# Sending the output stores of a batched matmul through the queue of its loads, and copying its sums out bank by bank

## The chip, the cores and the metric

One core of a Trainium2 chip. The metric is the device time of one execution in microseconds (us), as a median over runs. All runs compared here are fast: no execution was over 1.5% longer than the fastest of its kernel. One execution per run of each kernel was also profiled, and the traces are of those. The span of a profile is 1.8 us shorter than the time of its execution.

## The reference

```python
batch, m, k, n = 32, 512, 1024, 768
x      = randn(batch, m, k)   # float32
weight = randn(batch, k, n)   # float32
out    = np.matmul(x, weight) # float32
```

167.8 MB are read and 50.3 MB written, so there are 218.1 MB to move. Nothing is used twice.

## The kernel before

Loads go through GpSimd's (POOL) software queue, which casts float32 to bfloat16 on the way (a batch's 2048 KB of `x` land as 1024 KB, its 3072 KB of weights as 1536 KB). Stores go through SP's hardware queue, except those of the three batches before the last, which are held back behind all loads. The 128x128 blocks of `x` are transposed on PE.

```python
    CHUNKED = {B - 4: (4, 4), B - 3: (4, 4), B - 2: (4, 4), B - 1: (4, 2, 2)}
    HELD = {B - 4, B - 3, B - 2}
    # ... pools: w 5, x 5, xT 8, out 5 buffers; sums: 2 tiles of three PSUM banks ...

    def load_x(b):
        xs[b] = x_pool.tile([P, MT, K], BF16, name="x_sb")
        nc.gpsimd.dma_start(out=xs[b], in_=x_view[b])
    # ... load_w(b) the same, in the chunks of CHUNKED ...

    def evacuate(b, pair, pm):
        o = outs[b]
        nc.scalar.copy(o[:, pair * N2:pair * N2 + 1024], pm[:, 0:1024])
        nc.vector.tensor_copy(o[:, pair * N2 + 1024:(pair + 1) * N2], pm[:, 1024:N2])

        for b in range(B):              # loads of batches 0 to 3 were issued before
            if b + 4 < B:
                load_x(b + 4)
                load_w(b + 4)
            outs[b] = out_pool.tile([P, MT * N], F32, name="out_sb")
            if b not in CHUNKED:
                # ... transposes, matmuls, evacuate of two pairs of row tiles ...
                nc.sync.dma_start(out_view[b], outs[b])
                continue
            # ... last four batches: in the last chunk of batch b, the transposes
            #     of batch b + 1 stand between its matmuls ...
                        evacuate(b, pair, pms[pair])
                        if b not in HELD:       # the last batch: two half stores
                            cols = slice(pair * N2, (pair + 1) * N2)
                            nc.sync.dma_start(out_view[b, :, cols], outs[b][:, cols])
            if b in HELD:
                nc.gpsimd.dma_start(out=out_view[b], in_=outs[b])
```

## Time and profile before

| before | |
|---|---|
| time | 520.1 us, median of 3 (519.97 to 521.08) |
| span of the profile | 518.8 us |
| PE busy | 425.6 us (82%) |
| DMA work, 218.1 MB at the 428.2 GB/s of mid-span (428.9 with the instruction fetches) | 509.3 us |

The page's rows for the whole span: the busy tenths of the DMA engines in 40 slices, the two queues, and the transfers with their size and the median time from issue to landing.

```profile
DMA  8999999999999999999999999999999999999996
...
q0 software_dynamic: 10368, 88.61, 79.3%
q1 hardware_dynamic: 4320, 45.61, 21.2%
...
w_sb<-in_weight_dram POOLq DMA_DIRECT2D x28, 1536.0 KB, 63.1
out_dram<-out_sb SPq DMA_DIRECT2D x28, 1536.0 KB, 14.5
...
out_dram<-out_sb POOLq DMA_DIRECT2D x3, 1536.0 KB, 17.1
out_dram<-out_sb SPq DMA_DIRECT2D x2, 768.0 KB, 3.5
```

The DMA row is at its highest digit in all but the first and the last slice: this kernel is bound by the DMA engines. (The page's chain of work that ended last runs 80% through PE.) Queue 0 carries the loads (and the three held stores), queue 1 the other stores. A store that shares the engines with loads takes 14.5 us to land; a half store of the last batch, alone, takes 3.5.

The table of windows gives the same for stretches of time. The columns are the stretch, its length, busy time and instructions of PE, PEld, DVE, ACT and POOL, the clock granted to PE, the DMA share, and the GB/s written by the engines (a load counts with its bfloat16 bytes here).

```profile
core 0: us, PE busy (x) PEld busy (x) DVE busy (x) ACT busy (x) POOL busy (x), PEclk, DMA share, GB/s
260.00:300.00 40.00, 33.10 (x201) 21.93 (x203) 10.91 (x17) 6.08 (x6) 2.63 (x5) 0.96 1.02 261
500.00:505.00 5.00, 5.00 (x33) 3.09 (x32) 1.85 (x3) 1.01 (x1) 0.53 (x1) 1.00 0.99 412
505.00:510.00 5.00, 4.95 (x31) 3.04 (x31) 0.00 (x0) 0.00 (x0) 0.00 (x0) 1.00 0.87 369
510.00:515.00 5.00, 2.12 (x14) 1.08 (x12) 1.38 (x2) 2.02 (x2) 0.00 (x0) 1.00 0.41 168
515.00:518.80 3.80, 0.00 (x0) 0.00 (x0) 0.00 (x0) 0.00 (x0) 0.00 (x0) 0.61 0.58 238
```

In mid-span the share is 1.02, so there is no gap to fill. In the last 14 us it falls to 0.87, 0.41 and 0.58. The same stretch in finer slices (40 slices of 505 to 520 us, 0.375 us each):

```profile
DMA  9999898996563541200000698979999960000000
GB/s 393 393 459 459 360 459 360 492 459 295 229 262 164 229 197 66 98 0 0 0 0 0 262 426 360 492 311 475 393 426 426 360 262 0 0 0 0 0 0 0
```

The engines run out of held stores one after the other, all stand still for about 1.7 us, and then the last half stores run. By the packets of the trace, the last held store ends at 511.79 us on the slowest engine and the first half-store packet starts at 513.45: 1.66 us are lost even on the slowest engine.

The list of waits (engine, line, what it waited for: us in total, times, longest):

```profile
DVE out_sb L90 <- ACT out_sb L89: 157.7, 36, 8.4
...
PE pm L78 <- DMA w_sb<-in_weight_dram: 58.3, 21, 5.2
```

PE waits for weights because DMA bounds it. VectorE's long wait for ScalarE (one three-bank tile is copied out by both) is on an engine with time to spare (busy 124.2 of 518.8 us).

### The profile page before, as it was taken

Reading aid. Unit: us, or ns where it says so; the run is one execution under the profiler, and the core shown is the slowest. Engines: PE = TensorE matmul, PEld = TensorE weight load, DVE = VectorE, ACT = ScalarE, POOL = GpSimd, SP = SyncE. Lnnn points to the kernel's source line nnn. Section 1 sums busy time; section 2 is a strip of 40 time slices with the busy share of each in tenths; the row PEclk is TensorE's granted clock in tenths of the full one; section 3 lists DMA queues with packets and bytes.
Section 4 is the critical chain, followed back from the end, with each engine's and each line's share of the span. In section 5 each row is a group of like instructions: output and inputs, shape, how many; then the busy total and the mean of one; then the engine's idle time right before and its main releaser. Section 6 shows DMA issues by size and latency. Waiting matters only on the chain.

```text
span 518.8 us, 5796 instructions
## 1 busy us (share of the span) xinstructions
PE 425.6 (82%) x2512; PEld 278.3 (54%) x2560; DVE 124.2 (24%) x192; ACT 66.1 (13%) x65; POOL 38.9 (7%) x78
## 2 busy tenths in 40 slices
PE   1788789788888878897888978788887879878994
PEld 1455456455555545564555645466554555555662
DVE  1122222222221212212122122122221221223331
ACT  0011111011110101110011101011010110101111
POOL 4000000000000000000000000000000000001000
PEclk9999899798998979998899989799898997998998
DMA  8999999999999999999999999999999999999996
GB/s 159 216 231 268 269 265 277 275 239 272 254 275 278 253 270 241 275 279 273 253 250 262 275 279 247 268 250 275 277 252 273 242 273 278 265 266 229 215 329 250
DMA packets 14713, 134.59 MB, mean 259 GB/s; under 512 B 1632, under 2 KB 1632, under 8 KB 3040
## 3 DMA queue, kind: packets, MB, share of 16 engines
q0 software_dynamic: 10368, 88.61, 79.3%
q1 hardware_dynamic: 4320, 45.61, 21.2%
q8 instruction: 20, 0.33, 0.2%
q14 instruction: 5, 0.04, 0.0%
HBM read 167.77 MB, written 50.33 MB: 420 GB/s over the span
## 4 chain that ended last, share of the span: by engine, by line
PE 80%; another core or an unknown queue 10%; DMA 3%; issue 2%; ACT 2%; DVE 1%; POOL 0%; DVEq 0%; POOLq 0%
PE pm L78 70%; PE pt L64 11%; DMA w_sb<-in_weight_dram 3%; ACT out_sb L89 2%; DVE xT L66 1%; DVE out_sb L90 0%; POOL x_sb L50 0%; DVEq L66 0%; POOLq L152 0%
## 5 line engine op out<-in xcount | busy, mean ns | idle before, releaser
L78 PE MATMUL pm<-w_sb,xT 128*128 128x256 bf16 (+1 forms) x2000 | 372.4, 341 | 72.6 <-DMA w_sb<-in_weight_dram 58.3
L78 PEld LDWEIGHTS <-xT 128*128 128x128 bf16 x2048 | 207.6, 102 | 211.8 <-issue 56.5
L66 DVE COPY xT<-pt 128x1024 bf16<-128x1024 bf16 x128 | 85.2, 686 | 232.0 <-PE pt L64 232.0
L89 ACT COPY out_sb<-pm 128x1024 f32<-128x1024 f32 x64 | 64.8, 1013 | 446.3 <-PE pm L78 446.3
L64 PE MATMUL pt<-ident,x_sb 128*128 128x128 f32 x512 | 80.2, 291 | 13.9 <-DMA x_sb<-in_x_dram 12.5
L64 PEld LDWEIGHTS pt<-ident,x_sb 128*128 128x128 f32 x512 | 76.6, 207 | 21.6 <-issue 15.0
L90 DVE COPY out_sb<-pm 128x512 f32<-128x512 f32 x64 | 44.0, 687 | 157.7 <-ACT out_sb L89 157.7
L56 POOL DMA_DIRECT2D w_sb<-in_weight_dram x37 | 19.7, 531 | 239.2 <-DMA w_sb<-in_weight_dram 204.2
L50 POOL DMA_DIRECT2D x_sb<-in_x_dram x32 | 17.1, 536 | 196.8 <-PE pt L64 133.1
L137 POOL DMA_DIRECT2D out_dram<-out_sb x3 | 1.6, 533 | 29.2 <-DVE out_sb L90 29.2
L89 ACT ACT_TABLE_LOAD x1 | 1.3, 1283 | 0.7 <-PEq L152 0.7
masks.py:199 POOL TENSOR_SCALAR_AFFINE_SELECT ident<-ident 128x128 f32<-128x128 f32 x1 | 0.3, 287 | 0.1
masks.py:197 POOL MEMSET ident<- 128x128 f32 x1 | 0.2, 243 | 0.0
L152 POOL MEMSET const-float32-0.0<- 128x1 f32 x1 | 0.1, 99 | 0.2 <-issue 0.2
L152 POOL MEMSET const-bfloat16-1.0<- 128x1 bf16 x1 | 0.1, 102 | 0.0
L152 POOL MEMSET const-uint8-127<- 128x1 uint8 x1 | 0.1, 102 | 0.0
L152 POOL MEMSET const-float32-1.0<- 128x1 f32 x1 | 0.1, 99 | 0.0
## 6 DMA issues: line engine op xcount, KB each, us to landing
w_sb<-in_weight_dram POOLq DMA_DIRECT2D x28, 1536.0 KB, 63.1
out_dram<-out_sb SPq DMA_DIRECT2D x28, 1536.0 KB, 14.5
x_sb<-in_x_dram POOLq DMA_DIRECT2D x32, 1024.0 KB, 62.1
w_sb<-in_weight_dram POOLq DMA_DIRECT2D x7, 768.0 KB, 48.1
out_dram<-out_sb POOLq DMA_DIRECT2D x3, 1536.0 KB, 17.1
out_dram<-out_sb SPq DMA_DIRECT2D x2, 768.0 KB, 3.5
w_sb<-in_weight_dram POOLq DMA_DIRECT2D x2, 384.0 KB, 29.4
```

What stands on the lines that cost most here:

```text
L50: nc.gpsimd.dma_start(out=xs[b], in_=x_view[b])
L56: nc.gpsimd.dma_start(out=ws[b][:, at:at + n, :], in_=w_view[b, :, at:at + n, :])
L64: nc.tensor.transpose(pt[:, j, :], pairs[:, mt, j::JT], ident)
L66: nc.vector.tensor_copy(xT.rearrange("p j m r -> p (j m r)"), pt.bitcast(BF16).rearrange("p j m -> p (j m)"))
L78: nc.tensor.matmul(pm[:, half * N + off:half * N + off + size], xT[:, ko // 2, :, ko % 2], ws[b][:, ko, off:off + size], start=(ko == 0 an ...
L89: nc.scalar.copy(o[:, pair * N2:pair * N2 + 1024], pm[:, 0:1024])
L90: nc.vector.tensor_copy(o[:, pair * N2 + 1024:(pair + 1) * N2], pm[:, 1024:N2])
L137: nc.gpsimd.dma_start(out=out_view[b], in_=outs[b])
L152: nc = _bacc.Bacc("TRN2", target_bir_lowering=False, num_devices=1)
```

## The change

The intent is one queue that feeds the DMA engines in a fixed order: each store except the last batch's stands in the loads' queue, behind the load three batches ahead: the iteration of batch `b` issues the loads of `b + 3` and then the store of `b - 1`. For that, out buffers go from 5 to 7, load buffers from 5 to 4 and the look-ahead from four batches to three. The three-bank sum becomes three one-bank tiles, copied out by three copies.

```diff
-    HELD = {B - 4, B - 3, B - 2}
+    AHEAD = 3
-    ... w bufs=5, x bufs=5, out bufs=5
+    ... w bufs=4, x bufs=4, out bufs=7
+    def banks():
+        return [mpsum.tile([P, 512], F32, name=f"pm{i}") for i in range(3)]
 ... SPLITS and the matmuls' output name a bank and a column in it ...
     def evacuate(b, pair, pm):
-        o = outs[b]
-        nc.scalar.copy(o[:, pair * N2:pair * N2 + 1024], pm[:, 0:1024])
-        nc.vector.tensor_copy(o[:, pair * N2 + 1024:(pair + 1) * N2], pm[:, 1024:N2])
+        o = outs[b][:, pair * N2:(pair + 1) * N2]
+        nc.scalar.copy(o[:, 0:512], pm[0])
+        nc.vector.tensor_copy(o[:, 512:1024], pm[1])
+        nc.scalar.copy(o[:, 1024:N2], pm[2])
 ...
         for b in range(B):
-            if b + 4 < B:
-                load_x(b + 4)
-                load_w(b + 4)
+            if b + AHEAD < B:
+                load_x(b + AHEAD)
+                load_w(b + AHEAD)
+            if b > 0:
+                nc.gpsimd.dma_start(out=out_view[b - 1], in_=outs[b - 1])
 ...
-                nc.sync.dma_start(out_view[b], outs[b])
                 continue
 ...
-                        if b not in HELD:
+                        if b == B - 1:
 ...
-            if b in HELD:
-                nc.gpsimd.dma_start(out=out_view[b], in_=outs[b])
```

More of the change, by code (lines that the diff above doesn't have):

```diff
@@ L29 @@
     CHUNKED = {B - 4: (4, 4), B - 3: (4, 4), B - 2: (4, 4), B - 1: (4, 2, 2)}
-    HELD = {B - 4, B - 3, B - 2}
+    AHEAD = 3
     const = ctx.enter_context(tc.tile_pool(name="const", bufs=1))
-    w_pool = ctx.enter_context(tc.tile_pool(name="w", bufs=5))
-    x_pool = ctx.enter_context(tc.tile_pool(name="x", bufs=5))
+    w_pool = ctx.enter_context(tc.tile_pool(name="w", bufs=4))
+    x_pool = ctx.enter_context(tc.tile_pool(name="x", bufs=4))
     xT_pool = ctx.enter_context(tc.tile_pool(name="xT", bufs=8))
-    out_pool = ctx.enter_context(tc.tile_pool(name="out", bufs=5))
+    out_pool = ctx.enter_context(tc.tile_pool(name="out", bufs=7))
     tpsum = ctx.enter_context(tc.tile_pool(name="tpsum", bufs=2, space=bass.MemoryType.PSUM))
@@ L69, in transpose @@
         return xT
-    SPLITS = (((0, 512), (512, N - 512)), ((0, 1024 - N), (1024 - N, N2 - 1024)))
+    SPLITS = (
+        ((0, 0, 0, 512), (1, 0, 512, N - 512)),
+        ((1, N - 512, 0, 1024 - N), (2, 0, 1024 - N, N2 - 1024)),
+    )
     def matmuls(pm, half, xT, b, kos, together):
         for ko in kos:
-            for i, (off, size) in enumerate(SPLITS[half]):
+            for i, (bank, at, off, size) in enumerate(SPLITS[half]):
                 shares = half == 1 and i == 0
                 nc.tensor.matmul(
-                    pm[:, half * N + off:half * N + off + size],
+                    pm[bank][:, at:at + size],
                     xT[:, ko // 2, :, ko % 2],
@@ L96 @@
         make_identity(nc, ident)
-        for b in range(1, 4):
+        for b in range(1, AHEAD):
             load_x(b)
@@ L109 @@
                 for pair in range(2):
-                    pm = mpsum.tile([P, N2], F32, name="pm")
+                    pm = banks()
                     for half in range(2):
@@ L117 @@
                     evacuate(b, pair, pm)
-                nc.sync.dma_start(out_view[b], outs[b])
                 continue
             xT = ready.pop(b, None) or {mt: transpose(b, mt) for mt in range(MT)}
-            pms = [mpsum.tile([P, N2], F32, name="pm") for _ in range(2)]
+            pms = [banks() for _ in range(2)]
             at = 0
```

## The prediction

> **What bounds the kernel now.** The DMA engines, nearly everywhere. The page's DMA line reads 9 tenths in all slices but the first (8) and last (6); the table of windows gives a share of 1.02 to 1.03 in each 40 us stretch from 20 to 460 us. PE is busy 82% and waits 58.3 us for weights (list of waits). By packet sizes in the trace, counting a load by its float32 source bytes (twice what lands as bf16), the engines read about 428 GB/s wherever loads (first queue) and stores (second queue) mix. Loads alone reach 425 to 428 (4 to 30 us, 482 to 497 us); stores alone, held ones on the loads' queue, 405 to 420 (499 to 508 us), 0.46 us per 12 KB packet against 0.472 on the second queue. So mixing two queues costs nothing that separating could give back: 218.1 MB at 428 GB/s is 509.6 us of the 518.8 us span; the first packet starts at 2.6 us.
>
> **What lies outside that.** About 5 to 7 us, nearly all at the end. The held stores are done at 512.2 us, the last batch's half stores are issued at 512.6 and 513.9 us and land at 515.9 and 517.8 us: DMA share 0.87 (505 to 510), 0.41 (510 to 515), 0.58 after. But the engines are skewed: the 16 engines' landings of one late load spread over 3.5 to 6.4 us, and the slowest engine works until about 511.5 us. On it only 1.5 to 2 us is idle.
>
> **What the change does.**
> - Bytes, packets and matmuls are unchanged. 28 stores move from SP's queue to POOL's: 28 issues of 0.53 us on an engine 7% busy. [...] (a store beside loads lands after 14.5 us, though its bytes need 3.7 us alone).
> - The software queue has eight completion semaphores; weight loads are issued as the weights four batches back land. With three transfers per batch, eight in flight are 2.7 batches, about 42 us of DMA work: the queue should not run dry, although store b waits on POOL for batch b's evacuation.
> - Order: when the last weights land, 27 stores are done instead of 28, so they land about 3.7 us earlier, and four held stores (15 us) cover the last matmuls. The tail's idle time goes; the slowest engine gains its 1.5 to 2 us.
> - Evacuation by PSUM bank lets VectorE (0.69 us) go without waiting for ScalarE (1.01 us): up to 1 us before the last store, which now queues beside held stores anyway. The 157.7 us that VectorE waits for ScalarE are off the path.
> - Against: [...] POOL may be held by a wait.
>
> Net: minus 1 to 3 us for the tail, plus 0 to 3 for bubbles. I predict 518.3 us, 514.5 to 521.5; faster by over 2%: 0.02, within 2%: 0.94, slower: 0.04.
>
> **What would show it.** DMA share still 1.02 in mid-span; about 428 GB/s by source bytes; the last weights land near 497 us instead of 501; no 0.41 dip at the end; stores take 40 us or more to land; PE's wait for weights still about 58 us; VectorE's wait for ScalarE gone.
>
> **What would make it wrong.** The queue running dry because eight transfers or POOL's waits delay the next load; a mid-span rate below 420 GB/s because loads and stores no longer overlap in an engine; or above 432 because they no longer interfere; skew between engines growing or shrinking.

## The result, and the profile after

After: 517.88 us, median of 4 (517.62 to 518.26); before, on the same chip, 520.08 us. The ratio is 0.9954, 95% interval 0.9937 to 0.9971. (A ratio is the mean time of one kernel's fast runs over that of the other's of the same rounds, so it is not quite the ratio of the medians quoted.) Two later repetitions of after gave 517.70 (ratio 0.9938) and 518.00 us (0.9956). The predicted 518.3 us was near, and the class "within 2%" is right.

The page's rows for the whole span:

```profile
DMA  8999999999999999999999999999999999999996
...
q0 software_dynamic: 14400, 132.65, 99.9%
q1 hardware_dynamic: 288, 1.57, 0.7%
...
out_dram<-out_sb POOLq DMA_DIRECT2D x31, 1536.0 KB, 41.9
w_sb<-in_weight_dram POOLq DMA_DIRECT2D x28, 1536.0 KB, 43.2
...
out_dram<-out_sb SPq DMA_DIRECT2D x2, 768.0 KB, 7.0
```

Nearly everything is now on queue 0. A store takes 41.9 us from issue to landing, because it stands behind a load three batches ahead. The queue does not run dry: the DMA share is 1.02 to 1.03 in each 40 us stretch from 20 to 460 us. The trace bears out the prediction's eight: the landings of queue 0 are told on eight semaphores (99 to 106) and come in the order of issue, before and after, and counted at each issue there are never more than eight transfers in flight on it, the one issued included. In before there are eight at each issue from 5.6 to 479.2 us, and a weight load of mid-span is issued 0.53 us after the weights four batches back have landed; in after there are eight at each issue from 44.2 to 483.7 us. The last half stores take 7.0 us instead of 3.5: they are issued at 506.06 and 507.35 us, and held stores run beside them until 511.2 us.

The table of windows:

```profile
260.00:300.00 40.00, 34.52 (x212) 22.81 (x215) 9.89 (x15) 6.45 (x11) 4.25 (x8) 0.96 1.02 256
500.00:505.00 5.00, 4.95 (x32) 3.05 (x32) 0.00 (x0) 0.27 (x1) 0.00 (x0) 1.00 1.01 430
505.00:510.00 5.00, 1.70 (x11) 0.80 (x9) 1.38 (x2) 2.02 (x4) 0.00 (x0) 0.92 0.93 391
510.00:515.00 5.00, 0.00 (x0) 0.00 (x0) 0.00 (x0) 0.00 (x0) 0.00 (x0) 0.50 0.40 165
515.00:516.50 1.50, 0.00 (x0) 0.00 (x0) 0.00 (x0) 0.00 (x0) 0.00 (x0) 0.50 0.00 0
```

The finer slices of 505 to 520 us:

```profile
DMA  9996699989989795664232110000000000000000
GB/s 393 459 393 262 262 426 393 475 344 459 442 344 524 311 492 213 262 262 180 98 131 98 82 82 16 0 0 0 0 0 0 0 0 0 0 0 0 0 0 0
```

The gap is gone. The share of 510 to 515 us is still low (0.40, where the prediction expected no such dip), but it is no standstill. The long slope from 510 us on is the difference between the engines: the 16 landings of one late weight load are spread over 4.6 us here (3.8 us before), and the last digits belong to the slowest engines, which do not pause.

The waits:

```profile
DVE out_sb L97 <- PE pm L85: 116.2, 36, 8.5
...
PE pm L85 <- DMA w_sb<-in_weight_dram: 61.9, 23, 5.2
POOL w_sb L59 <- DMA out_dram<-out_sb: 56.5, 18, 3.2
```

VectorE no longer waits for ScalarE, and PE's wait for weights is about the same (61.9 against 58.3 us): this fits a copying out that is off the path, which e1 tests. GpSimd now waits 56.5 us for stores to land before it issues loads, and the DMA share does not fall for it (1.02 in 260 to 300 us, as before).

Two things in the trace were not in the prediction. First, counting a load by its source bytes (bfloat16 packets doubled, instruction fetches of 0.7 GB/s included), the engines move 430.3 GB/s between 60 and 450 us where they moved 428.9 before. Second, the program ends later after its last data packet: 2.24 us against 1.38. The end of the kernel, before and after, is a group of semaphore and drain instructions of one line; durations are min/median/max in ns, then the first and last start. Before:

```profile
L163 POOLq EVENT_SEMAPHORE  x4: 17/17/17, 518.1 to 518.7; - x4
L163 POOLq DRAIN  x3: 46/102/11436, 503.8 to 518.5; - x3
L163 SPq DRAIN  x3: 7/7/7, 518.0 to 518.3; - x3
```

After:

```profile
L170 POOLq EVENT_SEMAPHORE  x4: 17/17/17, 515.8 to 516.4; - x4
L170 POOLq DRAIN  x3: 46/95/18397, 497.3 to 516.2; - x3
L170 SPq DRAIN  x3: 7/7/7, 514.7 to 516.0; - x3
```

Before, SP has seen all stores land and drains at 518.0 us, and GpSimd follows at once (518.1): the last store ends the program. GpSimd's own long drain had ended at 503.77 + 11.44 = 515.2 us. After, SP is through at 514.7 us, but GpSimd's drain (from 497.34, 18.40 us long) ends only at 515.7, and the closing semaphores start at 515.8. The program's end has a new wait.

### The profile page after: what moved, and what is told of

Its sections match the earlier page's. It is cut to its first block, busy times and chain, and to the rows that moved or that the text cites. A ratio compares the mean times of both kernels' runs of the same rounds, so it can differ in the third digit from the quotient of the medians.

```text
span 516.5 us, 5888 instructions
## 1 busy us (share of the span) xinstructions
PE 424.2 (82%) x2512; PEld 277.7 (54%) x2560; DVE 127.0 (25%) x192; ACT 76.3 (15%) x129; POOL 53.9 (10%) x106
## 4 chain that ended last, share of the span: by engine, by line
DMA 74%; PE 21%; DVE 2%; issue 1%; ACT 0%; POOL 0%; POOLq 0%
DMA w_sb<-in_weight_dram 37%; DMA out_dram<-out_sb 24%; PE pm L85 19%; DMA x_sb<-in_x_dram 13%; PE pt L67 2%; DVE xT L69 1%; DVE out_sb L97 1%; ACT out_sb L98 0%; POOL x_sb L53 0%; POOLq L53 0%; POOLq L59 0%; POOLq L159 0%
## 5 line engine op out<-in xcount | busy, mean ns | idle before, releaser
L85 PE MATMUL pm<-w_sb,xT 128*128 128x256 bf16 (+1 forms) x2000 | 370.7, 340 | 66.6 <-DMA w_sb<-in_weight_dram 61.9
L96 ACT COPY out_sb<-pm 128x512 f32<-128x512 f32 x64 | 37.5, 586 | 287.9 <-PE pm L85 284.5
L98 ACT COPY out_sb<-pm 128x512 f32<-128x512 f32 x64 | 37.5, 586 | 142.4 <-PE pm L85 142.2
L53 POOL DMA_DIRECT2D x_sb<-in_x_dram x32 | 17.1, 536 | 192.6 <-DMA w_sb<-in_weight_dram 141.8
L59 POOL DMA_DIRECT2D w_sb<-in_weight_dram x37 | 19.7, 532 | 114.2 <-DMA out_dram<-out_sb 56.5
L115 POOL DMA_DIRECT2D out_dram<-out_sb x31 | 16.6, 536 | 136.8 <-DMA x_sb<-in_x_dram 64.7
## 6 DMA issues: line engine op xcount, KB each, us to landing
out_dram<-out_sb POOLq DMA_DIRECT2D x31, 1536.0 KB, 41.9
```

The costliest lines, as they stand in the source:

```text
L59: nc.gpsimd.dma_start(out=ws[b][:, at:at + n, :], in_=w_view[b, :, at:at + n, :])
L85: nc.tensor.matmul(pm[bank][:, at:at + size], xT[:, ko // 2, :, ko % 2], ws[b][:, ko, off:off + size], start=(ko == 0 and not (together an ...
L96: nc.scalar.copy(o[:, 0:512], pm[0])
L98: nc.scalar.copy(o[:, 1024:N2], pm[2])
L115: nc.gpsimd.dma_start(out=out_view[b - 1], in_=outs[b - 1])
```

## The experiments

The theory to test is that the gain is made of (a) the tail: stores deferred behind loads let PE finish earlier and cover its last work, worth the 1.66 us of idle time; and (b) a slightly higher rate in mid-span; while (c) the wait for GpSimd's drain takes part of it back. (c) was added after the runs e5 to e7. Rivals are the evacuation by bank, the buffers and look-ahead, and the tail alone.

All but the first of after were timed in 5 rounds. Source rate is as above, 60 to 450 us. The last three columns are read from the packets and instructions of the profiled execution: the last packet of the software queue, the last data packet of all, and the end of GpSimd's long drain.

| kernel | median us | ratio to before | GB/s | software queue ends | last packet | drain ends | span |
|---|---|---|---|---|---|---|---|
| before | 520.1 | 1 | 428.9 | 511.8 | 517.4 | 515.2 | 518.8 |
| after (first, again, third) | 517.9, 517.7, 518.0 | 0.9954, 0.9938, 0.9956 | 430.3 | 511.2, 510.8, 511.3 | 514.3, 514.5, 514.3 | 515.7, 515.3, 515.8 | 516.5, 516.0, 516.5 |
| e1_banks | 519.89 | 0.9986 | 428.9 | 512.0 | 518.7 | 515.3 | 520.1 |
| e2_hold_one_more | 518.71 | 0.9955 | 428.9 | 511.7 | 515.4 | 515.2 | 516.9 |
| e3_sp_stores | 519.00 | 0.9963 | 428.9 | 512.2 | 515.4 | 515.6 | 516.9 |
| e4_store_first | 519.76 | 0.9968 | 430.7 | 511.5 | 517.1 | 515.9 | 518.3 |
| e5_route_only | 519.39 | 0.9968 | 430.4 | 512.2 | 514.7 | 516.6 | 517.4 |
| e6_half_matmuls | 519.97 | 0.9979 | 430.6 | 513.3 | 513.8 | 517.8 | 518.5 |
| e7_last_on_pool | 521.55 | 1.0010 | 430.3 | 514.7 | 514.7 | 519.3 | 520.0 |
| e8_store30_late | 519.36 | 0.9979 | 430.4 | 507.1 | 517.5 | 511.5 | 518.8 |
| e9_half30_late | 517.69 | 0.9934 | 430.2 | 508.7 | 514.3 | 513.2 | 515.5 |

Before itself scatters, from 519.9 to 522.6 us over all its runs, which widens the intervals of the ratios to about 0.2% either way. The ratios of e2, e3 and after can't be told apart; the packets' times can, but they come from one profiled execution of each kernel (three of after).

### e1_banks: the evacuation alone

```diff
 (before)
-    pm = mpsum.tile([P, N2], F32, name="pm")
+    pm = banks()          # and SPLITS, matmuls, evacuate as in the change
```

> The kernel before with one part of the change alone: the sums of a pair of row tiles lie in three one-bank tiles and are copied out by three copies. Theory (the gain of 2.2 us is made of the order of the transfers at the end, about 1.7 us of idle time on the slowest DMA engine, and of about 1 to 2 us in mid-span from store packets that take 0.462 us on the software queue and 0.472 on the other): this part is off the path but for the last copies, 519.5 to 520.1 us. Rival (the evacuation by bank made the gain): about 518 us. VectorE's wait for ScalarE goes in either case; mid-span rate stays 429 GB/s by source bytes.

519.89 us, ratio 0.9986 with an interval of 0.9964 to 1.0008: no difference shown, and the theory's range held. The profiled execution was the longest of its six (521.85), because its last half stores came at 513.9 us; the median is what counts here. The evacuation by bank did not make the gain as far as the medians show; the interval alone would leave room for up to 1.9 us, and the stronger evidence is e5, which has after's rate and nearly its last packet without it.

### e2_hold_one_more: the tail alone

```diff
 (before)
-    HELD = {B - 4, B - 3, B - 2}
+    HELD = {B - 5, B - 4, B - 3, B - 2}
-                nc.sync.dma_start(out_view[b], outs[b])
+                (nc.gpsimd if b in HELD else nc.sync).dma_start(out_view[b], outs[b])
```

> The kernel before with one more store (of the fifth batch from the end) held on the loads' queue behind the last loads; all other stores stay on the second queue. Theory of the tail: the last weights land about 3.7 us earlier (497.4 us), no engine idles before the last half stores, 1.5 to 2 us gained: 518.2 to 518.7 us. If the gain came from mid-span alone: 519.9 to 520.1 us.

518.71 us (518.47 to 518.79), at the upper end of the theory's range. The rate is still 428.9 GB/s. The slices of 505 to 520 us:

```profile
DMA  9999999865699898999985543300000000000000
```

One more store held fills the gap, and the last packet ends at 515.42 us instead of 517.42. So the tail is worth 2.0 us, 1.66 of them the idle time. These two changed lines get most of what the whole change gets.

### e3_sp_stores: everything but the route of the stores in mid-span

```diff
 (after)
-            if b > 0:
+            if b > B - 5:
                 nc.gpsimd.dma_start(out=out_view[b - 1], in_=outs[b - 1])
 ...
                     evacuate(b, pair, pm)
+                if b < B - 5:
+                    nc.sync.dma_start(out_view[b], outs[b])
                 continue
```

> The kernel after, but the stores of batches 0 to 26 go through SP's second queue as soon as their batch is copied out; the four after them stay behind the last loads as in the change. Buffers, look-ahead and banks as after. Theory of the rate: store packets take 0.472 us again, mid-span rate falls from 430.8 to 429 GB/s, the time is 1 to 2 us above after (518.9 to 519.9 us), the tail is as after. If the tail alone made the gain: 517.9 us, as after.

519.00 us (518.85 to 519.29), within the range of the theory of the rate; the rate fell to 428.9 GB/s, and the last packet ended at 515.43, as in e2. Against after (514.25, 514.50 and 514.35 in its three profiles) the route costs 0.9 to 1.2 us of DMA time. The match in device time is partly luck: all six executions of e3 are 2.05 to 2.19 us longer than their spans, those of all other kernels 1.73 to 1.99, and the record doesn't show why; with the usual 1.8 us it would have been about 518.6, below the range. By the spans of all executions the route costs 0.75 us (median 516.85 against 516.1 of after's 15). e3 has after's buffers, look-ahead and banks, e2 has those of before, and on one chip, in the same rounds, both end alike (last packets 515.43 and 515.42 us): with the stores on SP's queue, these three parts bring nothing. Queue and moment of issue change together in e3, so it doesn't tell one from the other. In the packets, a 12 KB store packet of mid-span takes 472.3 ns here and 461.6 ns in after, while load packets are 0.2 to 0.3% shorter here. With eight data packets per store and engine, 27 stores come to 27 x 8 x 10.7 ns = 2.3 us, of which the shorter load packets take part back.

### e4_store_first: one store more ahead of the last loads

```diff
 (after)
+            if b > 0:
+                nc.gpsimd.dma_start(out=out_view[b - 1], in_=outs[b - 1])
             if b + AHEAD < B:
                 load_x(b + AHEAD)
                 load_w(b + AHEAD)
-            if b > 0:
-                nc.gpsimd.dma_start(out=out_view[b - 1], in_=outs[b - 1])
```

> The kernel after with the store of each batch issued ahead of that iteration's loads instead of behind them, so that 28 stores and not 27 go ahead of the last weights. Theory: rate as after (430.5 to 430.9 GB/s); last weights at about 500 us, three held stores keep the slowest engine busy until about 511 us, the half stores are issued at about 509.8 and 511: nearly no idle time, 517.9 to 518.6 us. If the number of stores behind the last weights is what matters by itself: 519.5 us or more.

The rate was as expected, but the time was 519.76 us: outside the theory's range and in the rival's. The half stores came at 512.2 us and not at 509.8, and all engines stood still from 511.5 to 513.1 us. The expectation had taken the last weights for what PE waits for. It is the last `x`: its transposes stand inside the last chunk of the batch before. The PE groups of that time:

```profile
478.20 1.46 PE L85 MATMUL pm<-w_sb,xT 128*128 128x512 bf16 x8
...
493.46 0.75 PE L67 MATMUL pt<-ident,x_sb 128*128 128x128 f32 x4 [3.27 <-DMA x_sb<-in_x_dram]
...
494.05 2.42 PE L85 MATMUL pm<-w_sb,xT 128*128 128x512 bf16 x8
...
497.12 1.81 PE L85 MATMUL pm<-w_sb,xT 128*128 128x256 bf16 x8
...
501.01 11.86 PE L85 MATMUL pm<-w_sb,xT 128*128 128x256 bf16 x72
...
512.23 1.63 SPq L143 DMA_DIRECT2D out_dram<-out_sb  x2
```

In after, 17.1 us pass from the first transpose of the last `x` (488.92 us) to the issue of the first half store (506.06), although the last weights had landed at 496.3. Here the last `x` is transposed at 493.46 us, 4.5 us later. And after that wait the first eight matmuls took 2.42 us where eight alike had taken 1.46 (478.20). PE had waited 3.27 us here and the granted clock was 0.83 between 490 and 500 us, while in after's first profile it had waited 1.12 us there, the clock stayed at 1.00 and such eight took 1.46 us. By the trace's clock records, half the clock was granted here for one stretch of 3.41 us (494.39 to 497.81). A wait of 2.96 us in before (until 468.32 us) came with such a stretch too (468.05 to 471.46). What sets the clock is not shown. After's second profile had such a wait as well (3.26 us) and half the clock from 488.77 to 492.18 us; its half stores came 1.6 us later than in the first, and it lost nothing, because its held stores lasted until 510.8 us. Two of the six runs of e4 took 517.9 and 518.5 us; they were not profiled, and why they escaped is open.

### e5_route_only: the order and the queue, in the kernel before

```diff
 (before)
             if b + 4 < B:
                 load_x(b + 4)
                 load_w(b + 4)
+            if 0 < b and b - 1 not in HELD:
+                nc.gpsimd.dma_start(out=out_view[b - 1], in_=outs[b - 1])
 ...
-                nc.sync.dma_start(out_view[b], outs[b])
                 continue
```

> The kernel before with the stores of batches 0 to 27 moved to the loads' queue, each behind the load four batches ahead; buffers (5, 5, 5), look-ahead of four, whole-tile sums and evacuation as before. Theory (queue and order make the whole gain, buffers, look-ahead and banks none): mid-span rate 430.3 to 430.9 GB/s by source bytes, no idle time between the held stores and the last half stores, 517.5 to 518.4 us, as after. If buffers, look-ahead or banks carry part of it: above 518.7 us.

The rate is after's (430.4), there is no gap, and the last packet ends at 514.70 us, 0.2 to 0.4 us later than in after. But the time is 519.39 us, which the expectation gave to the rival. The DMA work is not what differs: the last `x` now comes a store earlier, the half stores are issued at 505.6 us instead of 506.1 to 507.6, they share the engines with more of the held stores, and the software queue ends at 512.15 us instead of 510.8 to 511.3. GpSimd's drain then ends at 516.6, and the program 0.7 us later. So buffers, look-ahead and banks are not needed for the gain in DMA time. That the look-ahead of three pays here because it lets the software queue end a little sooner is read from the trace; no run changes it alone.

### e6_half_matmuls: PE with half of its work

```diff
 (after; wrong result on purpose)
         for ko in kos:
+            if ko % 2 == 1:
+                continue
-                    stop=(ko == KT - 1),
+                    stop=(ko == KT - 2),
```

> The kernel after with every second step of K left out (wrong result on purpose): half of the matmuls and weight loads, all transfers as after. If PE bounded any stretch, the time would fall by several us. Theory (the slowest DMA engine bounds all): PE falls from 424 to about 240 us busy, and the time hardly moves. Only instruction fetches become fewer (about 12 of 16 KB instead of 20, 0.93 us each on one engine): 0.5 us less on the mean engine, up to 2 us on the slowest if fetches make the skew between engines: 516.0 to 517.6 us, the spread of the 16 landings at the end below 3.5 us instead of 4.6 to 5.3.

The head of its page, with the span and the busy time of each engine:

```profile
span 518.5 us, 3888 instructions
...
PE 302.3 (58%) x1536; PEld 195.3 (38%) x1536; DVE 126.9 (24%) x192; ACT 76.0 (15%) x129; POOL 53.9 (10%) x106
```

519.97 us, above the expected range: with half of the matmuls the kernel is 2 us slower than after. (PE is busy 302 us and not 240; the mean granted clock was 0.79 instead of 0.94.) The DMA work did end earlier, at 513.75 us; 12 fetches of 16 KB instead of 20 are about the half us expected. But the half stores are issued at 500.5 us, 5.6 us before after's, so they share the engines with more of the held stores (11.0 us from issue to landing, against 7.0 in after). The software queue ends at 513.28, GpSimd's drain at 517.77, and the span at 518.5. All compute before the half stores ended early, and the program ended late: that was the sign that something waits for the software queue. The spread of the last landings did not shrink as expected (4.1 us at the last weights, 6.2 at the last held store). In after the spread of a load's 16 landings grows through the run, from 0.7 us at the first weights to 4.6 us at the last, and the trace has 20 packets of 16,384 bytes on the instruction queue, 0.93 us each. How much of the engines' difference comes from these fetches is open.

### e7_last_on_pool: the last half stores on the software queue too

```diff
 (after)
-                            nc.sync.dma_start(out_view[b, :, cols], outs[b][:, cols])
+                            nc.gpsimd.dma_start(out=out_view[b, :, cols], in_=outs[b][:, cols])
```

> The kernel after with the last batch's two half stores on the loads' queue too. Theory: the slowest engine has held stores queued until about 511 us either way, so the queue's longer way to its first byte costs nothing, and 16 packets a little shorter (0.231 instead of 0.240 us) save 0.15 us: 517.5 to 518.1 us. If the two queues side by side at the end are worth something, or the loads' queue starts late there: 518.5 us or more.

521.55 us, a clear miss. The last packet ends at 514.70 us, within 0.5 us of after's; the span ends 5.3 us after it. The half stores' packets were not shorter either: 240.8 ns, against 240.4 in before on SP's queue; the 231 expected are an estimate, half of the 462 ns that a 12 KB packet took on the software queue. (Of the queue's longer way to its first byte: 1.38 us pass here from the issue of the first load to its first packet, and 0.83 us in before from that of the first half store.) The slices of 505 to 520 us:

```profile
DMA  9996566543129999969999700000000000000000
```

The drains and closing semaphores at its end:

```profile
L170 POOLq EVENT_SEMAPHORE  x4: 17/17/17, 519.3 to 519.9; - x4
L170 POOLq DRAIN  x3: 46/82/9512, 509.7 to 519.7; - x3
L170 SPq DRAIN  x3: 7/7/7, 515.2 to 519.5; - x3
```

The engines have been silent from 514.7 us on, SP has seen everything land at 515.2, and GpSimd's drain, begun at 509.74, lasts 9.51 us, until 519.25. Over all 13 profiles this drain ends 4.4 to 4.6 us after the software queue's last packet where 99 to 102 transfers went through that queue, and 3.3 to 3.4 us where 72 or 73 did. What it does in that time the profile doesn't show; that it waits for the queue is concluded from these times.

### e8_store30_late and e9_half30_late: ending the software queue sooner

```diff
 (after, e8)
-            if b > 0:
+            if 0 < b < B - 1:
                 nc.gpsimd.dma_start(out=out_view[b - 1], in_=outs[b - 1])
 ...
                             nc.sync.dma_start(out_view[b, :, cols], outs[b][:, cols])
+                            if pair == 0:
+                                nc.sync.dma_start(out_view[b - 1], outs[b - 1])
 (after, e9)
+                n = N2 if b == B - 1 else MT * N
-                nc.gpsimd.dma_start(out=out_view[b - 1], in_=outs[b - 1])
+                nc.gpsimd.dma_start(out=out_view[b - 1, :, :n], in_=outs[b - 1][:, :n])
 ...
                             nc.sync.dma_start(out_view[b, :, cols], outs[b][:, cols])
+                            if pair == 0:
+                                nc.sync.dma_start(out_view[b - 1, :, N2:], outs[b - 1][:, N2:])
```

> The kernel after once more, as the anchor for the run beside it: 517.6 to 518.3 us. GpSimd's last drain ends 4.5 us after the software queue's last packet (so far 4.45 to 4.55 us in six kernels with 100 transfers on that queue) and is what the program's end waits for.

It held: 518.00 us, ratio 0.9956, and the drain ended 4.5 us after the queue's last packet.

> The kernel after with the store of batch 30 moved from the loads' queue to SP's, between the two half stores of batch 31, so that the software queue ends about 3 us earlier. Theory of the drain: DMA work and its end stay (last packet 514.3 to 514.6 us), software queue done at 508 to 509 us, GpSimd's drain at about 513 us, so the program ends 1.0 to 1.1 us after the last landing as in the kernel before: span about 515.5 us, time 0.3 to 0.8 us below after (517.0 to 517.4). If the program's end does not depend on when the software queue ends: as after. Also: the 12 KB packets of this store on the second queue run beside no load; if such a packet is slower by the queue, it takes 0.472 us again; if by the loads beside it, 0.461.

e8 took 519.36 us, a miss. The drain ended at 511.5 us, and the program 0.9 us after its last landing (1.0 to 1.1 expected), so it no longer waits for the drain. But the software queue was empty at 507.1 us, a us sooner than reckoned, PE came late (half stores at 509.0, again after matmuls at half the clock, from 488.19 to 495.02 us), and 2.8 us were idle on every engine: the tail's loss of before, and more. The 12 KB packets of this store took 466.8 ns, neither 461 nor 472, so whether the queue or the loads beside it make such a packet slower stays open. (That e7's half-store packets were no shorter on the software queue speaks against the queue alone.)

> The kernel after with only the second half of batch 30's store moved to SP's queue, between the half stores of batch 31. The first half stays on the loads' queue, which then ends at about 509 to 510.5 us, between after (511.0 to 511.3) and the run with the whole store moved (507.1). Theory (the end is the later of two: the last store's landing, and the software queue's end plus 4.5 us for GpSimd's drain; and the slowest engine must not idle before the half stores, which come between 506 and 509 us): no idle time where they come by 509, drain at 513.5 to 515 us, end 1.25 to 1.5 us after the last packet, 0.2 to 0.8 us below after (517.0 to 517.7 us); where they come later, as after. If the drain costs nothing: 517.8 to 518.2 us.

The slices of 505 to 520 us in e9:

```profile
DMA  5755399999999999999942110000000000000000
```

e9 leaves half of that store where it was. The dip at 505 to 506.5 us is of engines that ran ahead; the slowest never stops. The last packet ends at 514.28 us, the drain at 513.2, and the span at 515.5, the shortest of all profiles (but over all executions its spans are 515.5 to 516.6 us, and after's 515.7 to 516.9). The median of 517.69 us is at the upper end of the expected range, and only as low as the best of after's three (517.70 to 518.00). So the wait for the drain is gone in the trace, but a gain over after in time isn't shown.

The repetition of after on the chip of e5 to e7:

> The kernel after again, so that it shares its chip and its runs of before with the three that follow: 517.6 to 518.3 us, ratio to before 0.995.

It held: 517.70 us, ratio 0.9938.

## Why the prediction was right

The predicted time was 518.3 us and the measured 517.88. Point by point:

- **DMA bounds the kernel: right.** The share stayed at 1.02 to 1.03 in mid-span, and e6 shows that with half of the matmuls the last packet ends only 0.5 to 0.8 us sooner.
- **1.5 to 2 us of idle time on the slowest engine, removed by the order: right.** It was 1.66 us; e2, which changes only this, ends its packets 2.0 us earlier. The route to it was told inexactly: the last weights did land earlier (496.3 against 501.1 us, predicted 497), but PE's last stretch hangs on the last `x` (e4).
- **The queue does not run dry with eight in flight: right.** The trace shows eight in flight at each issue from 44.2 to 483.7 us, stores land after 41.9 us, and the DMA share is unchanged (1.02 to 1.03).
- **The evacuation is off the path: right** (e1).
- **"So mixing two queues costs nothing that separating could give back": this step failed.** The prediction itself had both durations, 0.46 and 0.472 us per store packet. In place of "0 to 3 for bubbles" (idle time between transfers, the author's guess, which no trace had shown), the one queue moved 430.3 instead of 428.9 GB/s, and e3 puts that at 0.9 to 1.2 us of DMA time gained (one profile of e3; whether by the queue itself is open). The term had the wrong sign.
- **A term was missing.** With the tail filled, the program's end passes from the last store to GpSimd's drain, 4.5 us after the software queue. That gave back 0.1 to 0.9 us: the span ends 1.5 to 2.2 us after the last packet, against 1.2 to 1.5 us where the drain is not last.

The sum: the last packet moved from 517.42 to 514.25 us, 3.2 us, made of 2.0 for the tail (e2) and about 1.2 for the rate (e2 and e3 against after). The end lost 0.9 us of it (2.24 against 1.38), which leaves the 2.3 us by which the spans differ. The prediction settled on minus 1.8 us, in effect a tail of about 2 and bubbles near zero. Two errors, of minus 1.2 and plus 0.9 us, nearly cancelled: the tail was understood, but that the number came so near is luck.

## What to carry to other kernels

When DMA is busy in every slice, ask only two things of a new order of transfers: does it change the length of a packet (472.3 against 461.6 ns for 12 KB of store in e3 and after), and is any engine, the slowest above all, idle near the end (1.66 us in before). Hold back just enough stores to cover the compute after the last load; one more held store did most of it here (2.0 of 3.2 us). And look at what ends the program after the last packet: a queue that ends late can cost more than its data (e7 takes 3.6 to 3.9 us longer than after, with the last packet within 0.5 us of the same), so let the queue with the slow closing (the software queue: GpSimd's drain ended 3.3 to 4.6 us after its last packet) finish first, if that leaves no engine idle (in e9's trace the wait is gone, though no gain in time was shown; in e8 idle engines cost more).
